# Products of the weighted sum held back by one block, in a hybrid attention block on one core

## The chip, the cores and the metric

The kernel runs on one core of one Trainium2 chip. Its engines are TensorE (PE in the profile; its weight loads are PEld), VectorE (DVE), ScalarE (ACT), GpSimd (POOL), and SyncE (SP), which issues most DMAs. The metric is the device time of one execution in microseconds (us), as the median of several runs.

## The reference

One decoder layer over 1024 tokens of width 1024. Eight heads of stick-breaking attention and eight heads of multi-head latent attention (MLA) share an input projection and an output projection; then come a gated MLP with a causal convolution and a gated input embedding. All is computed to float32 accuracy. The change touches only the last step of both attentions, the weighted sum of the values:

```python
# stick-breaking, per 128-query block
weights = where(strict, exp(log_sigmoid(z) + log_keep_after), 0.0)
outs.append(einsum('bhqk,bkhd->bqhd', weights, v[:, :end]))
# MLA, per 128-query block
probs = softmax(where(causal, s, -inf), axis=-1)
outs.append(einsum('bhqk,bkhd->bqhd', probs, v[:, :end]))
```

## The kernel before

*Precision.* Float32 operands are split into a high part (rounded to the matmul's type by a copy on ScalarE, line 93) and a low part (the difference, on VectorE, line 94), and matmuls of the parts are added up in PSUM. In the tile names an ending h or l tells them apart: th and tl are the high and low part of a transposed block of weights.

*Stages.* Up to 111 us the input is normed and the first projections are made. From 111 to 409 us runs the stick-breaking attention, from 409 to 691 us the MLA attention. After that come the second half of the output projection, the MLP and the embedding.

*Units.* Each attention is cut into 16 units: one head (e tells the two heads of a pair apart) and one half g of the queries, 512 of them, that is four query tiles of 128. A unit of half g has 4g + 4 key blocks of 128, so 4 or 8 blocks; the 16 stick-breaking units have 96 blocks together, as have the MLA units. The scores and weights of a unit (`sb_softmax`, `ml_softmax`) are made four query tiles w[i] at a time, one per step. In the stick-breaking attention a step has a scan on VectorE (line 649) and a product (line 651), in MLA a reduction (line 1078) and an exponential (line 1079).

*The weighted sum.* `weighted_sum` goes over the key blocks j of a unit. For each it transposes the weights of up to four query tiles on TensorE into one PSUM bank with the tag "tr" (line 461; there are two such banks), splits the bank into th and tl (lines 93 and 94), and adds two products, of v(j) with th and with tl (lines 475 and 476), to the PSUM tile av, of which there is one buffer. The transposes of block j + 1 are issued ahead of the products of block j. v(j) holds the high parts of 64 value columns beside the low parts, so that av has two halves. At the unit's end the halves are added: line 479 copies the lower half into tmp, line 481 adds the upper half and writes o. In MLA the reciprocal sums are spread over a "tr" bank, rb, by eight small matmuls (line 487), line 489 adds the halves and line 490 multiplies into o. tmp has the tag "tl" and so shares the two buffers of tl. A post function then issues the store of o on POOL's queue (line 680 for the stick-breaking pairs, line 1096 in MLA).

*What runs beside it.* `run_units` advances the softmax of the next unit by the blocks of the present one, and each block also calls `prepare.step()` (splitting of MLA keys, values and queries) and `fill.step(rate)`, which issues a piece of a list of filler work: the next pair's projections, the preparation of MLA (lines 576 to 582 copy its keys and values through the tile lt and store them), output projection, embedding, MLP.

*What sets the order.* The kernel is written in a framework that gives each instruction a priority from its place in the program and places all waits itself. A planner then lays out each engine's queue with modelled durations: an engine takes, among the instructions that are ready by the plan, the one with the lowest priority number. Filler work can be given a later priority by the numbers in `LATER`. On the chip each queue runs in the order of that plan.

Of the kernel before, what the change touches and what calls it, by code (L numbers as in the profile page):

```python
# [9 lines left out]
F32 = mybir.dt.float32  # L10
F32R = mybir.dt.float32r
I32 = mybir.dt.int32
AF = mybir.ActivationFunctionType
ALU = mybir.AluOpType
# [4 lines left out]
P = 128  # L19
# [4 lines left out]
H = 512  # L24
HD = 64
# [24 lines left out]
def tile_hybrid_block(ctx: ExitStack, tc: tile.TileContext, a: dict, out: bass.AP):  # L50
    nc = tc.nc
    act, dve, pool, pe, sp = nc.scalar, nc.vector, nc.gpsimd, nc.tensor, nc.sync
# [16 lines left out]
    ident_r = const.tile([P, P], F32R, name="ident_r")  # L69
# [16 lines left out]
    def nm(s):  # L86
        uid[0] += 1
        return f"{s}_{uid[0]}"

    def split(h, l, src, gain=None, on_pool=False):  # L90

        if gain is None:
            act.copy(h, src)  # L93
            (pool if on_pool else dve).tensor_tensor(l, src, h, ALU.subtract)  # L94
        else:
            act.activation(h, src, AF.Copy, scale=gain)
            dve.scalar_tensor_tensor(l, src, gain, h, ALU.mult, ALU.subtract)
# [97 lines left out]
    now = {}  # L195
# [83 lines left out]
    with tc.tile_pool(name="pre", bufs=1) as pre, \  # L279
# [155 lines left out]
        for _ in project(8, to_v(pairs[0]), (1,), vws):  # L435
# [3 lines left out]
    atb = sb_scope.enter_context(tc.tile_pool(name="attn_b", bufs=1, side="right",  # L439
                                              reuse_waits="tile"))  # L440
# [10 lines left out]
    def weighted_sum(u, p_, ptr, pav, rate):  # L451

        g, w, v = u["g"], u["w"], u["v"]
        av = pav.tile([P, H], F32, tag="av", name=nm("av"))
        last = 4 * g + 3

        def transposed(j):
            tr = one_bank(ptr, "tr")
            for i in range(max(4 * g, j), last + 1):
                c = (i - 4 * g) * P  # L460
                pe.transpose(tr[:, c:c + P], w[i][:, j * P:(j + 1) * P], ident)  # L461
            return tr

        nxt = transposed(0)
        for j in range(last + 1):
            lo = max(0, j - 4 * g) * P
            tr = nxt
            th = p_.tile([P, H], F32R, tag="th", name=nm("th"), bufs=2)
            tl = p_.tile([P, H], F32R, tag="tl", name=nm("tl"), bufs=2)
            split(th[:, lo:], tl[:, lo:], tr[:, lo:])  # L470
            if j < last:
                nxt = transposed(j + 1)
            prepare.step()
            fill.step(rate)
            pe.matmul(av[:, lo:], v(j), th[:, lo:], start=j == 0, stop=False)  # L475
            pe.matmul(av[:, lo:], v(j), tl[:, lo:], start=False, stop=j == last)  # L476
            yield
        t_ = p_.tile([HD, H], F32, tag="tl", name=nm("tmp"), bufs=2)
        act.copy(t_, av[HD:, :])
        if "rs" not in u:  # L480
            dve.tensor_tensor(u["o"], av[:HD, :], t_, ALU.add)
            return

        rb = one_bank(ptr, "tr")
        for i in range(4):
            for m, r in enumerate(u["rs"]):
                pe.matmul(rb[:HD, i * P:(i + 1) * P], r[:, i:i + 1].to_broadcast([P, HD]), ident_r,
                          start=m == 0, stop=m == 1)
        dve.tensor_tensor(t_, av[:HD, :], t_, ALU.add)
        dve.tensor_tensor(u["o"], t_, rb[:HD, :], ALU.mult)  # L490

    def run_units(units, softmax, p_, ptr, pav, rates):

        def start(u):
            u["pre"](u)
            return softmax(u)

        for _ in start(units[0]):
            pass
        for n, u in enumerate(units):  # L500
            nxt = start(units[n + 1]) if n + 1 < len(units) else iter(())
            per = 4.0 / (4 * u["g"] + 4) * AHEAD
            credit = 0.0
            for _ in weighted_sum(u, p_, ptr, pav, rates[u["g"]]):
                credit += per
                while credit >= 1.0:
                    credit -= 1.0
                    next(nxt, None)
            for _ in nxt:
                pass  # L510
            if u.get("post"):
                u["post"](u)


    def psum(name, bufs, side="left"):
# [3 lines left out]
    def one_bank(pool_, tag):  # L519
        return pool_.tile([P, H], F32, tag=tag, name=nm(tag))  # L520

    def cycle(makers):
        n = [0]

        def make():
            n[0] += 1
            return makers[(n[0] - 1) % len(makers)]()
        return make

    ptr = ctx.enter_context(tc.tile_pool(name="ptr", bufs=2, space=PSUM, reuse_waits="tile"))  # L530
    pav = ctx.enter_context(tc.tile_pool(name="pav", bufs=1, space=PSUM, reuse_waits="tile"))
# [1 line left out]
    x_cm, px = psum("px", 2)  # L533
    y_cm, py = psum("py", 2, "right")
    now["bank"] = cycle([lambda: one_bank(ppj, "pj")] + [lambda: one_bank(px, "pj")] * 2)
    now["tmp"] = lambda dt: atb.tile([P, H], dt, tag="lt", name=nm("lt"), bufs=4)

    def latent_t(j, th, lh, ll):
        src = tmp().rearrange("p (t c) -> p t c", t=4)
# [403 lines left out]
    with tc.tile_pool(name="mla", bufs=1, side="right", reuse_waits="tile") as ml:  # L943
# [20 lines left out]
        def load_q(pr):  # L964
            g, c = pr // 4, pr % 4
            t = mt("qld", [P, 4, 2 * QW], F32, 2)
            sp.dma_start(t, q_dram[c, :, 4 * g:4 * g + 4, :])
            loads["q", pr] = t

        def load_k(pr):  # L970
            g, c = pr // 4, pr % 4
            n = (g + 1) * H
            for e in range(2):
                t = mt("ld", [P, S], F32, 3)
                sp.dma_start(t[:HD, :n], k_dram[c, e * HD:(e + 1) * HD, :n])
                if 2 * pr + e - 8 * g < 3:
                    sp.dma_start(t[HD:QW, :n], kr_dram[:, :n])
                loads["k", 2 * pr + e] = t
# [8 lines left out]
        def make_k(n):  # L987
            t = loads.pop(("k", n))
            g = n // 8
            rows = QW if n - 8 * g < 3 else HD  # L990
            w = (g + 1) * H
            h, l = kts[n % 3]
            act.copy(h[:rows, :w], t[:rows, :w])
            yield
            pool.tensor_tensor(l[:rows, :w], t[:rows, :w], h[:rows, :w], ALU.subtract)
            yield

        def make_v(n):
            t = loads["v", n // 2]
            e, j = n % 2, 4 * (n // 8) + 4  # L1000
            z = ml.tile([P, NT, P], F32R, tag="v", name=nm("v"), bufs=3)
            src = t[:, :j, e * HD:(e + 1) * HD]
            act.copy(z[:, :j, :HD], src)
            pool.tensor_tensor(z[:, :j, HD:], src, z[:, :j, :HD], ALU.subtract)
            vs_[n] = z
            yield

        def make_q(n):
            t = loads["q", n // 2]
            e = n % 2  # L1010
            h, l = [mt("q" + x, [P, H], F32R, 2) for x in "hl"]
            ps = ptr.tile([P, H], F32, tag="tr", name=nm("tr"))
            for i in range(4):
                pe.transpose(ps[:QW, i * P:(i + 1) * P], t[:, i, e * QW:(e + 1) * QW], ident)
            act.activation(h[:QW], ps[:QW, :], AF.Copy, scale=MLA_SCALE)
            dve.scalar_tensor_tensor(l[:QW], ps[:QW, :], MLA_SCALE, h[:QW], ALU.mult,
                                     ALU.subtract)
            qs_[n] = (h, l)
            yield

        def ml_pre(u):
            n, e = u["n"], u["e"]
            pr = n // 2
            prepare.drain()
            if e == 0:
                ml_pre.o = ml.tile([P, H], F32, tag="o", name=nm("o"), bufs=2)
                for z in (n, n + 1):
                    prepare.add(make_v(z))
                if pr < 7:
                    load_k(pr + 1)  # L1030
                    load_q(pr + 1)
            elif pr < 7:
                for z in (n + 1, n + 2):
                    prepare.add(make_k(z))
            if n < 15:
                prepare.add(make_q(n + 1))
            if e == 1 and pr < 7:
                load_v(pr + 1)
            u["k"], u["q"] = kts[n % 3], qs_[n]
            u["v"] = lambda j: vs_[n][:, j, :]  # L1040
            u["out"] = ml_pre.o
            u["o"] = ml_pre.o[hs[e], :]
            g = u["g"]
            first = n == 0
            u["w"] = {i: (mq if first else ml).tile([P, (i + 1) * P], F32, tag=f"w{i % 4}",
                                                    name=nm(f"w{i}"), bufs=1 if first else 2)
                      for i in range(4 * g, 4 * g + 4)}
            if n == 8:
                y_cm[0].__exit__(None, None, None)
                y_cm[0], py_[0] = psum("py2", 1, "right")  # L1050
# [201 lines left out]
    for t in range(NT):  # L1252
# [7 lines left out]
        for n, (c0, c1) in enumerate(zip(cuts, cuts[1:])):  # L1260
            w = c1 - c0
            dh, o = c0 // 512, c0 % 512
# [19 lines left out]
        r = rstd_dve(rp, ssq[:, 0:1], D, 1, "rn", 4)  # L1282
# [65 lines left out]
```

## Time and profile before

| | |
|---|---|
| median of 3 runs | 1577.84 us (1576.06 to 1579.86) |
| the profiled execution | 1584.88 us, span 1583.1 us |
| TensorE busy | 1479.8 us, 93% of the span |
| VectorE busy | 1075.7 us, 68% |
| ScalarE busy | 841.2 us, 53% |
| mean granted TensorE clock | 0.978 |
| transposes of line 461 | 576, 102.6 us |
| products of lines 475 and 476 | 192 and 192, 78.5 and 77.2 us |
| th on ScalarE, tl on VectorE | 192 each, 91.0 and 103.2 us |

The profile is of one execution. Its times count from the span's start. A row of busy times by stretch gives the stretch, its length, and for each engine busy us and instructions, then the granted TensorE clock (1 is full speed), the DMA engines' share and GB/s. A row of waits names the waiting instruction by engine, tile and line, then what ended the wait, the total us, how many times, and the longest. A row in order of time gives the start, the duration, engine, line, operation, out<-in, shape and count, and in brackets the idle time of the engine before it with what ended it. A row of a group of one line gives minimum, median and maximum in ns and the first and last start in us; one of the groups by cost gives busy us and mean ns, then idle us before them.

### The profile page before, as it was taken

The page shows a single profiled execution, that of the slowest core. Times are in us where ns is not written, and L with a number is a line of the kernel's source. Part 1 is how long each engine was busy: PE and PEld are TensorE (multiplying, and loading weights), DVE is VectorE, ACT ScalarE, POOL GpSimd, SP SyncE. Part 2 cuts the span into 40 slices and gives each one's busy share as a digit, 9 for nine tenths or more (in the row PEclk, how much of TensorE's full clock was granted, in tenths as well). Part 3 has the DMA queues.
Part 4 walks back from the last instruction along what each step waited for, and adds up shares of the span by engine and source line. Part 5 has one row for each costly group of instructions (what it writes and reads, how often), then busy time and mean ns, then how long its engine had stood idle before and what let it go on. Part 6 is the DMA issues. An engine that isn't in the chain of part 4 may idle for free. (4 is left out here: it accounts for less than half of the span.)

```text
span 1583.1 us, 20827 instructions
## 1 busy us (share of the span) xinstructions
PE 1479.8 (93%) x7032; PEld 1212.8 (77%) x7032; DVE 1075.7 (68%) x2021; ACT 841.2 (53%) x1649; POOL 279.1 (18%) x319
## 2 busy tenths in 40 slices
PE   4998998987899898899999999999999999999996
PEld 3977886865678676777888788888888888888875
DVE  4559477899777767866658855445976656444798
ACT  5356465677777675655544544444544444444542
POOL 7106300002243334241114000000000000000033
PEclk9999999999899899999999999999999999999998
DMA  6031310113444424234435532223432222233354
GB/s 197 22 100 41 106 35 14 47 53 126 143 139 148 130 90 157 67 110 145 150 117 191 169 103 88 99 93 99 152 122 94 93 94 96 92 95 97 127 178 168
DMA packets 109212, 173.78 MB, mean 110 GB/s; under 512 B 10913, under 2 KB 47681, under 8 KB 109105
## 3 DMA queue, kind: packets, MB, share of 16 engines
q1 hardware_dynamic: 100400, 142.71, 28.7%
q0 software_dynamic: 8704, 29.74, 5.1%
q8 instruction: 55, 0.90, 0.2%
q14 instruction: 53, 0.43, 0.1%
HBM read 142.26 MB, written 30.15 MB: 109 GB/s over the span
## 5 line engine op out<-in xcount | busy, mean ns | idle before, releaser
L94 DVE TENSOR_TENSOR wl<-ws,wh 128x512 fp32r<-128x512 f32 x281 | 203.9, 727 | 147.4 <-ACT wh L93 84.2
L93 ACT CAST wh<-ws 128x512 fp32r<-128x512 f32 x296 | 182.9, 620 | 219.6 <-PE mm L897 103.4
L897 PE MATMUL mm<-bh,wh 128*128 128x512 f32 x456 | 180.1, 395 | 0.0
L895 PE MATMUL mm<-bh,wh 128*128 128x512 f32 x456 | 180.1, 395 | 0.0
L94 DVE TENSOR_TENSOR fl<-f,fh 128x512 fp32r<-128x512 f32 x88 | 60.8, 692 | 117.9 <-PE mm L118 77.4
L94 DVE TENSOR_TENSOR tl<-tr,th 128x512 fp32r<-128x512 f32 x192 | 103.2, 550 | 45.3 <-ACT th L93 41.8
L901 PE MATMUL mm<-bh,wl 128*128 128x512 f32 x456 | 126.0, 396 | 0.0
L93 ACT CAST th<-tr 128x512 fp32r<-128x512 f32 x192 | 91.0, 485 | 59.6 <-PE tr L461 49.5
L93 ACT CAST fh<-f 128x512 fp32r<-128x512 f32 x88 | 54.6, 622 | 110.0 <-PE mm L117 84.4
L1166 POOL DMA_DIRECT2D x_dram<-fd x8 | 4.3, 538 | 616.9 <-DVE fd L1165 584.0
L461 PE MATMUL tr<-ident,w 128*128 128x128 f32 x576 | 102.6, 286 | 10.5 <-DVE tl L94 5.7
L895 PEld LDWEIGHTS mm<-bh,wh 128*128 128x128 f32 x456 | 85.9, 188 | 19.9
L897 PEld LDWEIGHTS mm<-bh,wh 128*128 128x128 f32 x456 | 85.9, 188 | 19.8
L901 PEld LDWEIGHTS mm<-bh,wl 128*128 128x128 f32 x456 | 85.6, 188 | 19.8
L649 DVE TENSOR_TENSOR_SCAN kc<-kc,one_f 128x128 f32<-128x128 f32 (+3 forms) x64 | 88.0, 1381 | 13.1 <-ACT kc L646 12.9
L116 PE MATMUL mm<-wh,fh 128*128 128x512 f32 x242 | 95.6, 396 | 0.0
L476 PE MATMUL av<-tl,v 128*128 128x512 f32 x192 | 77.2, 404 | 19.4 <-DVE tl L94 18.1
L117 PE MATMUL mm<-wl,fh 128*128 128x512 f32 x242 | 95.3, 394 | 0.0
L461 PEld LDWEIGHTS tr<-ident,w 128*128 128x128 f32 x576 | 73.9, 146 | 26.4 <-DVE tl L94 8.6
L475 PE MATMUL av<-th,v 128*128 128x512 f32 x192 | 78.5, 409 | 12.9 <-ACT th L93 7.6
L118 PE MATMUL mm<-wh,fl 128*128 128x512 f32 x242 | 82.5, 395 | 0.0
L116 PE MATMUL pj<-hTh,wh 128*128 128x512 f32 x160 | 65.6, 410 | 0.0
(425 smaller groups left out, 3808.2 us busy)
## 6 DMA issues: line engine op xcount, KB each, us to landing
ws<-in_w_up SPq DMA_DIRECT2D x176, 256.0 KB, 2.6
ws<-in_w_down SPq DMA_DIRECT2D x88, 256.0 KB, 2.6
ws<-in_w_o SPq DMA_DIRECT2D x32, 256.0 KB, 2.8
xl<-x_dram SPq DMA_DIRECT2D x16, 512.0 KB, 4.1
ws<-in_w_in SPq DMA_DIRECT2D x24, 256.0 KB, 2.9
t<-o_dram SPq DMA_DIRECT2D x24, 256.0 KB, 3.2
xl<-o_dram SPq DMA_DIRECT2D x24, 256.0 KB, 2.9
xt<-in_x SPq DMA_DIRECT2D x8, 512.0 KB, 6.0
```

The costliest lines, as they stand in the source:

```text
L93: act.copy(h, src)
L94: (pool if on_pool else dve).tensor_tensor(l, src, h, ALU.subtract)
L116: pe.matmul(ps, lh, rh, start=start, stop=False)
L117: pe.matmul(ps, lh, rl, start=False, stop=False)
L118: pe.matmul(ps, ll, rh, start=False, stop=stop)
L461: pe.transpose(tr[:, c:c + P], w[i][:, j * P:(j + 1) * P], ident)
L475: pe.matmul(av[:, lo:], v(j), th[:, lo:], start=j == 0, stop=False)
L476: pe.matmul(av[:, lo:], v(j), tl[:, lo:], start=False, stop=j == last)
L649: dve.tensor_tensor_scan(rev, rev, one_f[:, 0:1].to_broadcast([P, n]), 1.0, ALU.mult, ALU.mult)
L895: pe.matmul(ps, wh[:, k * P:(k + 1) * P], nh[:, kk], start=kk == 0, stop=False)
L897: pe.matmul(ps, wh[:, k * P:(k + 1) * P], nl[:, kk], start=False, stop=False)
L901: pe.matmul(ps, wl[:, k * P:(k + 1) * P], nh[:, kk], start=False, stop=kk == NK - 1)
```

## The change

The products of block j are no longer issued in the step of block j. They are put into a list `held` and issued in the step of the next block, after that block's split, after the transposes of block j + 2, and after `prepare.step()` and `fill.step(rate)`. This goes across units: the products of a unit's last block, and with them the unit's end and its post function, are issued in the first step of the next unit, and those of the last unit after the loop. The tile av is taken only after that. th gets a third buffer; for the room, lt goes from four buffers to three and the MLA tile o from two to one.

```diff
 def weighted_sum(u, p_, ptr, pav, rate):
-    av = pav.tile([P, H], F32, tag="av", name=nm("av"))
...
+    def product(j, lo, th, tl):
+        pe.matmul(av[:, lo:], v(j), th[:, lo:], start=j == 0, stop=False)
+        pe.matmul(av[:, lo:], v(j), tl[:, lo:], start=False, stop=j == last)
+        if j == last:
+            finish()
+
+    def finish():
+        t_ = p_.tile([HD, H], F32, tag="tl", name=nm("tmp"), bufs=2)
+        act.copy(t_, av[HD:, :])
+        if "rs" not in u:
+            dve.tensor_tensor(u["o"], av[:HD, :], t_, ALU.add)
+        else:
+            rb = one_bank(ptr, "tr")
+            for i in range(4):
+                for m, r in enumerate(u["rs"]):
+                    pe.matmul(rb[:HD, i * P:(i + 1) * P], r[:, i:i + 1].to_broadcast([P, HD]),
+                              ident_r, start=m == 0, stop=m == 1)
+            dve.tensor_tensor(t_, av[:HD, :], t_, ALU.add)
+            dve.tensor_tensor(u["o"], t_, rb[:HD, :], ALU.mult)
+        if u.get("post"):
+            u["post"](u)
+
     nxt = transposed(0)
     for j in range(last + 1):
...
-        th = p_.tile([P, H], F32R, tag="th", name=nm("th"), bufs=2)
+        th = p_.tile([P, H], F32R, tag="th", name=nm("th"), bufs=3)
         tl = p_.tile([P, H], F32R, tag="tl", name=nm("tl"), bufs=2)
         split(th[:, lo:], tl[:, lo:], tr[:, lo:])
         if j < last:
             nxt = transposed(j + 1)
         prepare.step()
         fill.step(rate)
-        pe.matmul(av[:, lo:], v(j), th[:, lo:], start=j == 0, stop=False)
-        pe.matmul(av[:, lo:], v(j), tl[:, lo:], start=False, stop=j == last)
+        if held:
+            held.pop()()
+        if j == 0:
+            av = pav.tile([P, H], F32, tag="av", name=nm("av"))
+        held.append(lambda a=(j, lo, th, tl): product(*a))
         yield
...
+held = []
 def run_units(units, softmax, p_, ptr, pav, rates):
...
-        if u.get("post"):
-            u["post"](u)
+    held.pop()()
...
-now["tmp"] = lambda dt: atb.tile([P, H], dt, tag="lt", name=nm("lt"), bufs=4)
+now["tmp"] = lambda dt: atb.tile([P, H], dt, tag="lt", name=nm("lt"), bufs=3)
...
-            ml_pre.o = ml.tile([P, H], F32, tag="o", name=nm("o"), bufs=2)
+            ml_pre.o = ml.tile([P, H], F32, tag="o", name=nm("o"), bufs=1)
```

More of the change, by code (lines that the diff above doesn't have):

```diff
@@ L474, in weighted_sum @@
             fill.step(rate)
-            pe.matmul(av[:, lo:], v(j), th[:, lo:], start=j == 0, stop=False)
-            pe.matmul(av[:, lo:], v(j), tl[:, lo:], start=False, stop=j == last)
-            yield
[L478 to L490, printed above, removed]
+            if held:
[3 more added lines that the diff above has]
+            held.append(lambda a=(j, lo, th, tl): product(*a))
+            yield
+    held = []
     def run_units(units, softmax, p_, ptr, pav, rates):
```

## The prediction

> **What bounds the kernel now.** I read the page's busy times first, then the busy time by stage, then the waits of TensorE in the two attention stages, then the rows in order of time around typical waits.
>
> ```profile
> PE 1479.8 (93%) x7032; PEld 1212.8 (77%) x7032; DVE 1075.7 (68%) x2021; ACT 841.2 (53%) x1649; POOL 279.1 (18%) x319
> ```
>
> ```profile
> core 0: us, PE busy (x) PEld busy (x) DVE busy (x) ACT busy (x) POOL busy (x), PEclk, DMA share, GB/s
> 111.00:409.00 298.00, 267.66 (x1369) 219.45 (x1368) 236.53 (x313) 187.96 (x415) 53.14 (x79) 0.95 0.17 57
> 409.00:691.00 282.00, 251.81 (x1414) 210.87 (x1414) 207.15 (x390) 189.23 (x404) 105.30 (x93) 0.95 0.40 125
> 260.00:280.00 20.00, 15.74 (x68) 12.76 (x69) 12.86 (x19) 9.36 (x19) 0.00 (x0) 0.83 0.08 26
> 355.00:396.00 41.00, 31.49 (x155) 23.52 (x153) 40.94 (x53) 28.98 (x66) 12.18 (x17) 0.92 0.35 126
> ```
>
> TensorE is the bound. The change touches only the stick-breaking stage (111 to 409 us) and the MLA stage (409 to 691). There TensorE idles 298.00 − 267.66 = 30.3 and 282.00 − 251.81 = 30.2 us, 60.5 together, and its granted clock is 0.95, so some 0.05 × 580 = 29 us more go to half-rate stretches. So all that can be won is idle and slow clock in these 580 us; filler matmuls moved about win nothing, since their total stays. From 355 to 396 us VectorE is busy 40.94 of 41 us: there it is the bound.
>
> ```profile
> engine line waited for: us in total, times, longest us
> PE av L476 <- DVE tl L94: 12.2, 18, 1.4
> PE tr L461 <- DVE tl L94: 5.0, 4, 2.1
> PE av L475 <- DVE o L481: 4.7, 2, 2.3
> PE av L475 <- ACT th L93: 0.3, 1, 0.3
> ...
> PE av L475 <- ACT th L93: 7.3, 5, 2.0
> PE av L476 <- DVE tl L94: 5.9, 8, 2.5
> PE tr L461 <- DVE o L490: 1.6, 2, 0.9
> PE tr L461 <- DVE tl L94: 0.7, 2, 0.4
> ...
> PE av L476 <- DVE tl L94: 4.3, 6, 1.4
> PE av L475 <- DVE o L481: 2.3, 1, 2.3
> PE tr L461 <- DVE tl L94: 0.9, 1, 0.9
> ```
>
> The waits of TensorE: four rows of 111 to 409, four of 409 to 691, three of 355 to 396 (part of the first). The first eight are the weighted sum's own: 12.2 + 5.0 + 4.7 + 0.3 = 22.2 and 7.3 + 5.9 + 1.6 + 0.7 = 15.5, so **37.7 of the 60.5 us**. Of these 4.3 + 2.3 + 0.9 = 7.5 lie where VectorE is full, and I leave them where they are.
>
> ```profile
> 378.66 0.60 PE L461 MATMUL tr<-ident,w 128*128 128x128 f32 x4
> 379.01 0.48 PE L475 MATMUL av<-th,v 128*128 128x512 f32 x1
> 379.75 0.66 DVE L94 TENSOR_TENSOR tl<-tr,th 128x512 fp32r<-128x512 f32 x1
> 380.46 0.50 PE L476 MATMUL av<-tl,v 128*128 128x512 f32 x1 [0.97 <-DVE tl L94]
> 380.79 0.60 PE L461 MATMUL tr<-ident,w 128*128 128x128 f32 x4
> ```
>
> One block in order of time. The product of th at 379.01 already stands behind the next block's transposes (378.66); the product of tl waits 0.97 us for VectorE (380.46), and the transposes of the block after that follow at 380.79. They need the same tl, since there are two "tr" banks and tl is the last reader of one. So whichever comes first on TensorE's queue takes the wait.
>
> **The change part by part.**
>
> *Product one block later.* Nothing is added or removed on any engine: 2 products, 4 (or fewer) transposes, one th and one tl per block as before; the program's order decides a priority, and the planner lays each engine's queue out by its own durations. What changes where TensorE waits for tl: the transposes of block j+2 go at once when tl(j) is there, and the products of block j stand behind them. The loop transposes, th, tl, transposes gets shorter by the slot that the product had in front: 380.79 − 380.46 = 0.33 us. Outside the full stretch there are 18 + 8 − 6 = 20 such waits, together 12.2 + 5.9 − 4.3 = 13.8 us: 20 × 0.33 = **−6.6 us** (bounds: 0, if only the name of the waiter changes, and −13.8, if the wait is wholly covered). The five waits for th in MLA (7.3 us) go the same way, as the next step needs tl too: 5 × 0.33 = **−1.7 us** (0 to −7.3).
>
> *The unit's end one block later, across units.*
>
> ```profile
> 262.46 2.28 DVE L649 TENSOR_TENSOR_SCAN kc<-kc,one_f 128x1024 f32<-128x1024 f32 x1
> 262.60 0.44 PE L461 MATMUL tr<-ident,w 128*128 128x128 f32 x2 [1.76 <-DVE tl L94]
> 264.66 0.66 DVE L481 TENSOR_TENSOR o<-av,tmp 64x512 f32<-64x512 f32 x1
> 265.37 0.80 PE L475 MATMUL av<-th,v 128*128 128x512 f32 x1 [2.33 <-DVE o L481]
> ```
>
> There is one av bank. The next unit's first product waits until o has read it, and o stood behind a scan of 2.28 us on VectorE: 2.33 us idle. The change puts the first product a block later, but the copy, the addition and (in MLA) the eight reciprocal matmuls come a block later too, behind the next unit's first split. Of the 4.7 − 2.3 = 2.4 us of such waits outside the full stretch, and of the 1.6 for L490, where rb holds a "tr" bank that the next unit's second block now gets first, I take three quarters: **−3 us** (bounds: −4.0, all of it; above, the second rival's +2.33 a unit end).
>
> *Clock.* Idle falls by 11.3 of 60.5 us, 19%; the same share of 29 us would be 5.4. The granted clock falls in steps (0.83 in 260 to 280, with 4.1 us of idle close together), so small gains may free none: I take half, **−3 us** (0 to −5.4).
>
> The Trainium skill, "TensorE: Matmul & The Clock Gate", section "Why this matters for your kernels", asks for no idle gap over some 3 us to keep the full clock. The longest wait here is 2.5 us, so by that rule alone the clock term would be 0 and the forecast 1571; the trace disagrees, with 0.83 around waits of 1.76 and 2.33 us.
>
> *The room for a third th buffer.* "lt" goes from 4 buffers to 3, MLA's "o" from 2 to 1.
>
> ```profile
> L581 DVE COPY lt<-pj x8: 656/680/684, 349.8 to 375.4; 128x512 f32<-128x512 f32 x8
> L576 ACT COPY lt<-pj x8: 578/614/658, 349.9 to 375.4; 128x512 f32<-128x512 f32 x8
> DMA to landing us min/median/max: 1.9/2.8/5.2
> ...
> L1096 POOL DMA_DIRECT2D o_dram<-o x8: 557/558/590, 436.9 to 692.8; - x8
> ...
> DMA to landing us min/median/max: 2.3/2.4/4.1
> ```
>
> Sixteen copies into lt in 25.6 us, 1.6 us apart. A slot is held for copy, issue and landing, about 0.68 + 0.56 (as the issue of o below) + 2.8 = 4.0 us, so three slots give one per 1.3 us: enough in the mean, not at the longest landing. It lies in the stretch where VectorE is full, and the work ends 33 us before the stage does: **+1 us** (0 to +3). MLA's o is stored 8 times, landing after 2.4 us (at most 4.1), and is written next about a unit later, 282 / 16 = 17.6 us: **0**; without that cover 8 × 2.4 = 19 us would be at stake, but it would need POOL to hang 13 us.
>
> *"tl" keeps two slots, which tmp shares.* At a unit's end tl(0) of the next unit and tmp hold both; tl(1) waits for o, now emitted after tl(0). Behind tl(1) on VectorE stand the next score reductions or scans, and ScalarE and TensorE wait for those.
>
> ```profile
> L481 DVE TENSOR_TENSOR o<-av,tmp 64x512 f32<-64x512 f32 x16 | 10.9, 678 | 1.5 <-ACT tmp L479 1.3
> ...
> L489 DVE TENSOR_TENSOR tmp<-av,tmp 64x512 f32<-64x512 f32 x16 | 10.9, 679 | 3.5 <-ACT tmp L479 3.5
> ```
>
> VectorE idled 1.5 + 3.5 = 5.0 us before these 32 operations, the first that each unit's end puts on it. A little over half of that again is added: **+3 us** (0 to +5.0; the rival has more).
>
> *Stores and the queues.* POOL issues the stores of o a block later; the fillers that unit 7 of MLA adds come a block later too. The last product and end of each of the two runs were the tail of them before as well. Nothing waits for these: **0**, bounded by one block in each run, 298 / 96 = 3.1 us.
>
> Sum: −6.6 − 1.7 − 3 − 3 + 1 + 3 = **−10.3 us**. The profiled execution took 1584.9 us (span 1583.1 and 1.8 around it) and would take 1574.6. It is 7.0 above the median of the three runs, 1577.84, so for the median I say **1568**.
>
> **The rivals.**
>
> *The wait only changes its name (no change).* Products already stand behind the next block's transposes (378.66 before 379.01), the transposes need the same tl, and where the planner has something else ready it puts it there in both versions. For it: the two "tr" banks are as they were, and the chain is bound by VectorE and ScalarE. Against it: the 2.33 us at 265.37 are not of that kind. Then only the clock's noise and lt's +1 stay: 1575 to 1580.
>
> *The later end blocks the next unit (slower).* Place: o on VectorE at each of the 32 unit ends. It is now emitted behind the last scores of the next unit and its first split, so more often a scan like that of 262.46 is put in front of it; the av bank, both tl slots and, in MLA, one "tr" bank hang on it. Price: 2.33 us for each, as at 265.37. Against the gains without that term, 6.6 + 1.7 + 3 − 1 = 10.3, it decides from 10.3 / 2.33 = 5 more unit ends on. If ten are hit: +23 − 10 = +13, so 1591; with seven, 1584.
>
> The Trainium skill, "TensorE: Matmul & The Clock Gate", "Architectural detail", says that VectorE and ScalarE are strictly first in, first out, so an o placed behind a scan cannot pass it. The trace agrees: o starts at 264.66, where the scan of 262.46 with 2.28 us ends.
>
> *The queue gets real slack (much faster).* If a block of delay covers all of 37.7 − 7.5 = 30.2 us, half of the 60.5, and the clock follows with half of its 29: −45, so 1533; half of that success is 1555. For it: waits of 0.4 to 2.5 us against a block of 3 us. Against it: the transposes' need of tl.
>
> **How the numbers follow.** A measurement of this kernel tells a change from none at about 0.2%, 3.2 us. The forecast (3 to 20 us faster, 1558 to 1575) gets 0.42, no change 0.20, the blocked unit ends 0.28, real slack 0.10. Faster is 0.42 + 0.10 = 0.52, within 0.2% 0.20, slower 0.28. The range leaves out the outer parts of the last two, about 0.1 each: 1552 to 1588.
>
> **What would show it.** Right: the waits of av for tl and th in the two stages fall from 26 and 6 to a few, some return as tr waiting for tl, and the sum of the eight rows falls from 37.7 to about 26; idle from 60.5 to about 50; clock 0.96. Products stand behind two later transposes rather than one. The name-change rival shows as tr waiting for tl by as much as av lost. The unit-end rival shows as av or tr waiting for o, or VectorE's tl waiting for o, in more than five unit ends. The forecast is wrong if the planner's new order moves fillers so that waits appear at lines which the change doesn't touch, or if lt's lost buffer is missed and waits of pj for lt take the place of those of av.

## The result, and the profile after

The changed kernel takes 1591.38 us in the median of four runs (1590.11 to 1604.27), the kernel before 1577.76 us (four runs, 1576.06 to 1579.86). The ratio is 1.0105, with a 95% interval of 1.0079 to 1.0131: **slower by 13.6 us**, where 10 us faster was forecast. The profiled execution took 1590.11 us, span 1588.3.

Busy time by stage, after (columns as before):

```profile
core 0: us, PE busy (x) PEld busy (x) DVE busy (x) ACT busy (x) POOL busy (x), PEclk, DMA share, GB/s
111.00:409.00 298.00, 263.27 (x1349) 217.12 (x1347) 231.09 (x311) 185.04 (x412) 54.23 (x79) 0.96 0.18 58
409.00:691.00 282.00, 247.48 (x1412) 206.87 (x1412) 208.77 (x392) 188.69 (x402) 100.08 (x90) 0.95 0.41 126
260.00:280.00 20.00, 15.91 (x75) 13.03 (x74) 11.25 (x16) 9.76 (x20) 0.00 (x0) 0.91 0.09 26
```

TensorE's idle time in the two stretches is now 34.7 and 34.5 us, 69.2 instead of 60.5. It should have fallen to about 50. The attention's last product starts earlier than before (682.2 instead of 689.1), but between 111 and 691 us TensorE was busy for 8.7 us less, with 22 matmuls fewer by the counts in the rows. So less filler was done beside the attention, and it comes after.

Over the whole execution the page gives

```profile
PE 1474.5 (93%) x7032; PEld 1210.6 (76%) x7032; DVE 1075.9 (68%) x2021; ACT 840.6 (53%) x1649; POOL 279.4 (18%) x319
```

that is 1588.3 − 1474.5 = 113.8 us idle against 1583.1 − 1479.8 = 103.3: 10.5 us more, with the same number of instructions on every engine. This one execution is only 5.2 us longer than that of before, because TensorE was 5.3 us less busy. Half of that is explained: it spent 65.0 us of its span at half rate, instead of 70.5, which is 2.7 us less of work lost. Where the other half comes from is not shown.

The four runs of the changed kernel have granted clocks of 0.980, 0.970, 0.979 and 0.974; the mean is 0.976, while the 79 runs of the kernel before that stand beside the experiments have a mean of 0.979. Time times one minus the clock estimates what half rate costs: 38.7 and 32.9 us. So of the difference of the means of these runs, 1594.3 − 1578.3 = 16 us, **about 6 is half-rate clock and about 10 is idle** by this estimate. The 6 hang on the one run at 0.970; the other three alone give 2.6.

The waits of TensorE, after, from 111 to 409 us and then from 409 to 691:

```profile
engine line waited for: us in total, times, longest us
PE tr L460 <- DVE tl L94: 15.2, 18, 2.2
PE av L464 <- DVE o L473: 6.8, 5, 2.3
PE pj L116 <- DVE v L94: 3.9, 2, 2.1
PE pj L116 <- ACT qt L620: 3.3, 2, 3.0
...
PE sc L656 <- ACT w L661: 1.8, 3, 1.3
...
PE tr L460 <- DVE tl L94: 7.3, 5, 2.2
PE tr L460 <- ACT w L1093: 3.3, 2, 2.0
PE sc L1084 <- ACT qh L1029: 3.2, 4, 2.6
PE av L464 <- ACT th L93: 3.2, 3, 1.4
PE sc L1084 <- ACT w L1093: 3.0, 4, 1.5
```

The products' waits for tl (18.1 us in 26 waits over both stretches) are nearly gone. The transposes now wait 15.2 + 7.3 = 22.5 us for the same tl, where they waited 5.0 + 0.7 before: **the wait changed its name**. In sum over all waits for tl of the weighted sum it is 23.8 us before (18.1 + 5.7) and 24.0 after (22.5, with 0.7 at the products and 0.8 at the reciprocal matmuls). The wait for o grew from 4.7 us (2 times) to 6.8 (5 times), the wait for th fell from 7.6 to 3.2. What else is new stands at lines that the change doesn't touch. With the rows of the two stages added up by kind, the scores waited 2.9 us in all and now 8.0, the fillers 13.6 and now 15.7, the transposes for w 2.7 and now 5.1.

One block in order of time, after (rows left out):

```profile
380.69 0.66 DVE L94 TENSOR_TENSOR tl<-tr,th 128x512 fp32r<-128x512 f32 x1
381.41 0.66 PE L460 MATMUL tr<-ident,w 128*128 128x128 f32 x4 [0.75 <-DVE tl L94]
381.82 0.49 PE L465 MATMUL av<-tl,v 128*128 128x512 f32 x1
382.15 0.40 PE L464 MATMUL av<-th,v 128*128 128x512 f32 x1
```

tl of 380.69 is waited for by the transposes that want its bank (0.75 us). The product at 381.82, right behind them, takes the same tl: counted in order, both are the 78th of 192. In the block shown of before, the product of the awaited tl stood first and had the wait (0.97 us). So a block later in the program is not a block later on the chip. In the median a product with tl starts 1.45 us after the end of its tl, where it started 0.96 us after it before.

VectorE's waits from 111 to 691 us, before and then after:

```profile
DVE mx L1078 <- PE sc L449: 10.9, 10, 2.2
...
DVE tl L94 <- PE av L476: 2.5, 2, 1.5
```

```profile
DVE mx L1092 <- PE sc L449: 15.5, 20, 3.0
...
DVE tl L94 <- PE av L465: 6.5, 6, 2.6
```

VectorE's reductions wait for scores twice as often. tl waits 6.5 us (6 times) for the held product that still reads its slot; before that was 2.5 us (2 times).

A unit's end, the first one of the stick-breaking attention, in order of time. First before, then after:

```profile
124.31 0.58 ACT L479 COPY tmp<-av 64x512 f32<-64x512 f32 x1
126.20 0.68 DVE L481 TENSOR_TENSOR o<-av,tmp 64x512 f32<-64x512 f32 x1
...
134.21 0.39 PE L475 MATMUL av<-th,v 128*128 128x512 f32 x1
```

```profile
132.59 1.13 ACT L93 CAST th<-tr 128x512 fp32r<-128x512 f32 x2
...
134.46 0.68 DVE L94 TENSOR_TENSOR tl<-tr,th 128x512 fp32r<-128x512 f32 x1
134.73 0.58 ACT L471 COPY tmp<-av 64x512 f32<-64x512 f32 x1
...
137.07 0.67 DVE L473 TENSOR_TENSOR o<-av,tmp 64x512 f32<-64x512 f32 x1
...
137.80 0.80 PE L464 MATMUL av<-th,v 128*128 128x512 f32 x1 [1.59 <-DVE o L473]
```

The last product of this unit ended at about the same time in both (it started at 123.21 before and at 123.74 after). Before, the end was over by 126.9 and the next unit's first product found av free 7 us later. After, tmp stands behind the next unit's split. That split had to wait for the next unit's weights, so av stayed taken until 137.7. Over the stick-breaking units tmp starts 4.15 us after the start of the unit's last product in the mean (0.90 before), in MLA, its last unit left out, 2.31 (1.05).

### The profile page after: what moved, and what is told of

Same layout as the page of the kernel before. It is cut to its first block, busy times and chain, and to the rows that moved or that the text cites. A ratio compares the mean times of both kernels' runs of the same rounds, so it can differ in the third digit from the quotient of the medians.

```text
span 1588.3 us, 20883 instructions
## 1 busy us (share of the span) xinstructions
PE 1474.5 (93%) x7032; PEld 1210.6 (76%) x7032; DVE 1075.9 (68%) x2021; ACT 840.6 (53%) x1649; POOL 279.4 (18%) x319
## 5 line engine op out<-in xcount | busy, mean ns | idle before, releaser
L460 PEld LDWEIGHTS tr<-ident,w 128*128 128x128 f32 x576 | 70.3, 145 | 51.6 <-DVE tl L94 33.5
L663 DVE TENSOR_TENSOR_SCAN kc<-kc,one_f 128x128 f32<-128x128 f32 (+3 forms) x64 | 87.3, 1369 | 13.1 <-ACT kc L660 12.8
L464 PE MATMUL av<-th,v 128*128 128x512 f32 x192 | 73.8, 384 | 11.9 <-DVE o L473 6.8
```

Of the source, the lines that this page charges most:

```text
L663: dve.tensor_tensor_scan(rev, rev, one_f[:, 0:1].to_broadcast([P, n]), 1.0, ALU.mult, ALU.mult)
```

## The experiments

Theories after the result. *Blocked unit ends*: the loss is the later unit end. *Later products inside a unit*: the loss is the place of the product behind two blocks' transposes. *Buffers*: it is lt, o, th or the slots. *Planner's scatter*: any reordering of these queues by the planner costs this much, whatever it is for. The expectations call the first two theory 1 and theory 2, and the last one theory 3. Each run has five rounds, beside runs of the kernel before on the same chip; a difference is between the two medians. What half rate costs is estimated each time as above, from the means of time times one minus the clock.

**Delay inside the units alone.** The unit's last products and its end are issued in their old place.

```diff
             held.append(lambda a=(j, lo, th, tl): product(*a))
+            if j == last:
+                held.pop()()
             yield
```

> The delay inside a unit alone: the last block's products and the unit's end are issued in the unit's own last step again; the third th buffer and the lost lt and o buffers stay. Theory 1 (the loss comes from the unit's end, which waits for the next unit's first split): the loss of 13.6 us goes, and what is left is the delay inside the unit, between 0 and -7 us: 1571 to 1578. The copy tmp starts about 1 us after a unit's last product (before 0.90 and 1.05 us in the mean, after 4.15 and 2.31). Theory 2 (the delay itself lengthens the wait, since the transposes take it over): still 8 to 14 us slower, 1586 to 1592, with tr waiting for tl by some 22 us. Theory 3 (any new order of the planner costs about as much): anywhere from 1575 to 1592.

Measured: 1590.18 against 1577.02, **+13.2 us**, ratio 1.0096 (1.0074 to 1.0118). tmp starts 1.02 and 1.10 us after the start of the last product, close to before. The whole loss is there without one late unit end, so blocked ends are not needed for it. Its runs have a mean clock of 0.9745 against 0.979, so more than half of this loss, 7.7 us, is half-rate clock.

**Delay across the unit ends alone.** Every product but a unit's last is issued at once.

```diff
             held.append(lambda a=(j, lo, th, tl): product(*a))
+            if j < last:
+                held.pop()()
             yield
```

> The delay at the unit's end alone: only the products of a unit's last block, and the unit's end, go into the next unit's first step; all other products are issued in their own step as before. Theory 1: the whole loss stays, 1588 to 1594, the copy tmp starts 2 to 4 us after a unit's last product, and av waits for o by about 7 us. Theory 2: close to the kernel before, 1576 to 1580, and TensorE waits for tl at the products again. Theory 3: anywhere from 1575 to 1592.

Measured: 1595.57, **+18.6 us**, ratio 1.0124 (1.0103 to 1.0144). So this half loses too, and the halves don't add up: 13.2 + 18.6 = 32 against 13.6 for both. The clock is part of it: with a mean of 0.973, some 10 of the 18.6 us are half rate. What the rest is made of was not taken apart.

**The buffers alone.** The kernel before with

```diff
-    now["tmp"] = lambda dt: atb.tile([P, H], dt, tag="lt", name=nm("lt"), bufs=4)
+    now["tmp"] = lambda dt: atb.tile([P, H], dt, tag="lt", name=nm("lt"), bufs=3)
-                ml_pre.o = ml.tile([P, H], F32, tag="o", name=nm("o"), bufs=2)
+                ml_pre.o = ml.tile([P, H], F32, tag="o", name=nm("o"), bufs=1)
```

> The kernel before with lt at three buffers and the MLA tile o at one; no product moves. Theories 1 and 2: within 2 us of before, 1576 to 1580. If the lost buffers make the loss: 1586 to 1592, with pj waiting for lt, or o for its store. Theory 3: up to 8 us away, as far as the planner's order changes.

Measured: 1582.56, **+5.5 us**, ratio 1.0030 (1.0015 to 1.0044).

**Buffers, taken apart: lt alone.** o with one buffer leaves the planned queues as they are, row by row, so only lt was run: the first two lines of the diff above.

> The kernel before with lt at three buffers alone; the MLA tile o keeps two. The queues are those of the run with both lost buffers, row by row, so if that run's 5.5 us come from lt: 1580 to 1585 again, and if they come from o's store at run time: 1575 to 1579.

Measured: 1583.13 against 1579.32, **+3.8 us**, ratio 1.0025 (1.0010 to 1.0041). The copies through lt are spread wider. Before:

```profile
L581 DVE COPY lt<-pj x8: 656/680/684, 349.8 to 375.4; 128x512 f32<-128x512 f32 x8
```

and with lt 3:

```profile
L581 DVE COPY lt<-pj x8: 661/678/692, 349.8 to 379.3; 128x512 f32<-128x512 f32 x8
```

The last copy comes 3.9 us later from the same start. So the room for the third th slot has a price of about 4 us in the kernel before.

**The whole delay with the buffers of before.** The changed kernel, and lt and o as in the lines with a minus above.

```diff
-            th = p_.tile([P, H], F32R, tag="th", name=nm("th"), bufs=3)
+            th = p_.tile([P, H], F32R, tag="th", name=nm("th"), bufs=2)
```

> The whole delay, inside units and across them, with the buffers of before: lt at four, the MLA tile o at two, th at two. The lost buffers alone cost 5.5 us, and the changed kernel 13.6. Theory 2 (two additive parts, the buffers and the order): 8 us slower than before, 1585, with TensorE's wait for tl at the transposes instead of the products. Theory 1 (all of the order's loss at the unit's end): the same 8 us, but with av waiting for o more than before's 4.7 us. If the third th buffer matters: 1590 or more.

Measured: 1592.21 against 1579.32, **+12.9 us**, ratio 1.0080 (1.0057 to 1.0104). Against the +13.6 of the changed kernel no difference can be seen: either the third th slot wins back what the lost lt slot costs, or the 4 us of lt are not added on top of the delay. No run tells these apart.

**tmp gets a buffer of its own** (the changed kernel, th with two).

```diff
-            t_ = p_.tile([HD, H], F32, tag="tl", name=nm("tmp"), bufs=2)
+            t_ = p_.tile([HD, H], F32, tag="tm", name=nm("tmp"), bufs=1)
```

> The changed kernel with a buffer of its own for tmp, for which th goes back from three buffers to two. Theory 1, in the form that tmp is held up because it takes its turn at the two tl slots behind the next unit's tl(0): tmp starts about 1 us after the last product, the second split of a unit no longer waits for o, and 6 to 12 us come back: 1579 to 1585. If the lateness lies in the program's order and not in the slots: 1588 to 1594, and tmp still starts 2 to 4 us late. Theory 2: no change against the changed kernel, 1588 to 1594.

Measured: 1586.71, **+9.7 us**, ratio 1.0059 (1.0044 to 1.0073). The same unit end as above:

```profile
123.34 0.58 ACT L471 COPY tmp<-av 64x512 f32<-64x512 f32 x1
125.22 0.68 DVE L473 TENSOR_TENSOR o<-av,tmp 64x512 f32<-64x512 f32 x1
...
133.48 0.39 PE L464 MATMUL av<-th,v 128*128 128x512 f32 x1
```

tmp no longer stands behind the next split, and the first product waits for nothing. In the mean over the stick-breaking units tmp starts 1.20 us after the start of the last product, and a unit's tl(1) starts 0.33 us after its tl(0) has ended, instead of 3.59 (1.57 in the kernel before). So the late end has a cause, the slots that tmp shares with tl, in which it takes its turn by place in the program. Mending it wins back 13.6 − 9.7 = 3.9 us of the loss, not all, and less than the 6 to 12 expected. The two differences come from separate comparisons, and th has two buffers here instead of three, so the 3.9 is rough.

**Two reorderings with no purpose.** The kernel before, first with the next unit's softmax advanced faster, then with other filler rates. The expectations count moved rows in the planned queue. In the traces, outside the longest order that each shares with the kernel before, stand 277 of TensorE's 7032 matmuls in the first and 804 in the second, against 825 in the changed kernel.

```diff
-AHEAD = 0.9
+AHEAD = 1.0
```

> The kernel before with the softmax of the next unit advanced a little faster (1.0 instead of 0.9 of a step per quarter of the unit); no product moves in the program, but the planner moves 518 of TensorE's 6326 rows. Theory 3 (the loss comes from any new order, since the numbers of before suit its own order): 3 to 12 us slower, 1580 to 1589, with waits spread over many lines. Theories 1 and 2 say nothing on it; within 3 us of before, 1574 to 1580, would speak against theory 3.

```diff
-SB_RATE = 0.75
-ML_RATE = (1.2, 0.8)
+SB_RATE = 0.7
+ML_RATE = (1.1, 0.7)
```

> The kernel before with fillers issued a little more slowly (0.70 instead of 0.75 per block in the stick-breaking stage, 1.1 and 0.7 instead of 1.2 and 0.8 in MLA); no product moves in the program, the planner moves 1091 of TensorE's rows, as many as the change does (1436). Theory 3: 3 to 12 us slower, 1580 to 1589. Within 3 us of before, 1574 to 1580, would speak against theory 3.

Measured: 1577.06 and 1578.15 against 1579.32, −2.3 and −1.2 us, ratios 0.9984 (0.9966 to 1.0001) and 0.9990 (0.9976 to 1.0005). In these two runs moving up to as many rows costs nothing, so a reordering by the planner does not cost this much whatever it is for.

**Inside the units, with the buffers of before.** As the first run, with th, lt and o as in the whole delay with the buffers of before.

> The delay inside a unit alone, with all buffers of before (th two, lt four, o two). Theory 2 (the transposes take over the wait for tl, so nothing is won, and the queue behind them gets worse): the run with the lost buffers was 13 us slower, of which lt's is 4 to 5; so 6 to 10 us slower, 1585 to 1589. TensorE's waits for tl together (at products and transposes) stay at 22 to 26 us, most of it at the transposes. Theory 1 (all of the loss at the unit's end): within 3 us of before, 1576 to 1582.

**The same, with the held product ahead of the next transposes.**

```diff
         split(th[:, lo:], tl[:, lo:], tr[:, lo:])
+        if held:
+            held.pop()()
         if j < last:
             nxt = transposed(j + 1)
         prepare.step()
         fill.step(rate)
-        if held:
-            held.pop()()
```

> As the run before it, but the held product is issued ahead of the next block's transposes instead of behind them and the fillers: the delay reaches over the softmax step and the next split alone. Theory 2: close to the kernel before, 1576 to 1582, with TensorE's waits for tl at the products again. If the delay over the split is what costs (ScalarE and VectorE rather than TensorE): as slow as the run before it, 1585 to 1589.

Measured, on one chip: 1594.19 and 1582.27 against 1578.41, **+15.8 and +3.9 us**, ratios 1.0102 (1.0078 to 1.0127) and 1.0030 (1.0012 to 1.0047). Waits of TensorE from 111 to 691 us, first behind and then ahead of the transposes:

```profile
PE tr L460 <- DVE tl L94: 18.8, 26, 2.5
PE sc L1085 <- ACT qh L1030: 6.9, 5, 5.7
PE av L464 <- ACT th L93: 6.2, 7, 1.6
PE av L464 <- DVE o L473: 5.9, 3, 2.3
PE av L465 <- DVE tl L94: 4.9, 8, 1.5
```

```profile
PE av L465 <- DVE tl L94: 18.7, 24, 2.4
PE tr L460 <- DVE tl L94: 5.6, 5, 2.1
PE av L464 <- DVE o L473: 4.8, 3, 2.3
...
PE av L464 <- ACT th L93: 2.9, 7, 0.7
...
PE sc L1085 <- ACT qh L1030: 1.7, 2, 1.6
```

The waits for tl are 18.8 + 4.9 = 23.7 and 18.7 + 5.6 = 24.3 us: equal, with the names exchanged. The 12 us lie elsewhere. All of TensorE's waits here are 68.5 and 56.9 us; 6.0 of the 11.6 between them are the scores' (10.3 and 4.3) and 3.3 are the products' for th. In the slower kernel the scores wait 6.9 us for qh alone, once 5.7, and VectorE's reductions wait for them:

```profile
DVE mx L1093 <- PE sc L449: 24.4, 18, 5.2
```

```profile
DVE mx L1093 <- PE sc L449: 15.2, 14, 2.7
```

These two kernels differ in one place in the program. If the product is put behind the transposes but ahead of `prepare.step()` and `fill.step(rate)`, the planned queues are those of the first of the two, row by row. So **it is the place behind the next transposes that costs, and the filler's place doesn't matter**. The clock changes little here: of the 12 us some 2 are half rate.

**A third tl slot.** The first run, and

```diff
-        th = p_.tile([P, H], F32R, tag="th", name=nm("th"), bufs=3)
-        tl = p_.tile([P, H], F32R, tag="tl", name=nm("tl"), bufs=2)
+        th = p_.tile([P, H], F32R, tag="th", name=nm("th"), bufs=2)
+        tl = p_.tile([P, H], F32R, tag="tl", name=nm("tl"), bufs=3)
```

> The delay inside a unit, with th at two buffers and tl at three, lt at three and o at one; the same with th at three and tl at two was 13.2 us slower than before. If the two tl slots are what binds (VectorE's in-order queue stands while a put-back product still holds one): 5 to 10 us come back, 1581 to 1586, and VectorE's wait of tl for products goes to about 0. If not: 1588 to 1595 as there.

Measured: 1590.59 against 1578.41, +12.2 us, ratio 1.0081 (1.0066 to 1.0096), where the first run had +13.2. VectorE's wait of tl for products, 3.8 us in the first run, is gone, and the loss is still there. So VectorE's wait for a slot that the held product still reads is not what costs.

**A third "tr" bank in the stick-breaking stage**, taken from the three banks of the fillers, in the kernel before and with the whole delay (buffers of before). Every third "tr" tile goes to pz; the lines of the class that does this are left out.

```diff
-    x_cm, px = psum("px", 2)
+    x_cm, px = psum("px", 1)
+    z_cm, pz = psum("pz", 1)
...
-    run_units(units, sb_softmax, atb, ptr, pav, (SB_RATE, SB_RATE))
+    run_units(units, sb_softmax, atb, Three(), pav, (SB_RATE, SB_RATE))
```

> The kernel before with a third tr bank in the stick-breaking stage, taken from the fillers' banks (three to two there). It is the reference for the next run. The fillers lose a bank, so 0 to 10 us slower, 1578 to 1588; the waits of products for tl in that stage fall a little from 12.2 us, and those of transposes for tl (5.0 us) go.

> The whole delay with the buffers of before, with a third tr bank in the stick-breaking stage. Theory 2 says that the delay fails there because the transposes need the same tl as the products, for want of a third bank: in that stage the waits for tl then fall by half or more against the reference run with three banks, and idle there is 4 us or more below that of the run with the delay and two banks (33.9 us). In the MLA stage nothing changes, so the whole is still slower than its reference, by 2 to 8 us. If the waits for tl in the first stage do not fall: the bank is not what binds, and the loss is that without the third bank, some 13 us.

Measured: 1588.93 and 1599.21 against 1578.41, +10.5 and +20.8 us, ratios 1.0063 (1.0040 to 1.0086) and 1.0131 (1.0109 to 1.0152). The fillers' lost bank costs 10.5 by itself, and the delay still costs 10.3 on top of it. By the clocks (means of 0.976 and 0.971) some 7.6 of these 10.3 are half rate. Waits in the stick-breaking stage, without and then with the delay:

```profile
PE av L476 <- DVE tl L94: 8.5, 12, 1.4
PE tr L461 <- DVE tl L94: 5.8, 6, 1.9
```

```profile
PE av L465 <- DVE tl L94: 7.7, 14, 1.1
...
PE tr L460 <- DVE tl L94: 6.2, 5, 1.6
```

14.3 and 13.9 us. The third bank takes 17.2 (12.2 + 5.0) down to 14.3, but with it the delay hides none of the rest. It does change who waits: with the delay and two banks the transposes had 13.4 us of such waits, with three they have 6.2, and the products 7.7. These products wait for their own tl and start 0.06 us after it, so the planned queue puts no block between a tl and its product here either. The lack of a third bank is not why the delay wins nothing.

**One stage alone** (inside the units, buffers of before): stick-breaking, then MLA.

```diff
-            if j == last:
+            if j == last or "n" in u:        # stick-breaking alone
+            if j == last or "n" not in u:    # MLA alone
                 held.pop()()
```

> The delay inside a unit with the buffers of before, in the stick-breaking stage alone; the MLA units issue each product in its own step. Idle of TensorE rose by 1 us in that stage and by 8.5 in MLA in the run with both, so: 2 to 6 us slower than before, 1580 to 1584. If each stage pays half: 1585 to 1588.

> The delay inside a unit with the buffers of before, in the MLA stage alone. By the idle of the run with both: 9 to 14 us slower than before, 1587 to 1592, with scores and fillers waiting 8 us or more longer in that stage. If each stage pays half: 1585 to 1588.

Measured: 1587.01 and 1579.10 against 1578.41, **+8.6 and +0.7 us**, ratios 1.0051 (1.0034 to 1.0068) and 1.0007 (0.9996 to 1.0017). Their sum, 9.3, is less than the 15.8 of both. It was expected the other way round, with most of the loss in MLA. TensorE's row from 409 to 691 us, MLA alone and then both:

```profile
409.00:691.00 282.00, 252.21 (x1419) 209.68 (x1420) 207.46 (x390) 187.67 (x399) 105.90 (x94) 0.95 0.41 126
```

```profile
409.00:691.00 282.00, 243.34 (x1380) 202.75 (x1380) 205.18 (x387) 186.01 (x396) 96.20 (x86) 0.95 0.39 123
```

The same MLA code idles 29.8 us behind the old stick-breaking stage and 38.7 behind the delayed one; the old MLA code behind the delayed stage idles 282.00 − 249.93 = 32.1. So what the delay costs in MLA depends on what the planner carries over from the stage ahead. **What stays open** is the carrier of the 15.8 − 9.3 = 6.5 us that the two stages cost only together, and of the scores' longer waits. The runs show that the loss comes with the product behind two blocks' transposes, and more from the stick-breaking stage, but not which planned instruction carries it; no run held the MLA queue equal while the stage ahead of it changed.

## Why the prediction was wrong, point by point

**The product one block later (−6.6 and −1.7 forecast).** This is the step that failed first. It took it that a loop of transposes, th, tl, transposes gets shorter by the product's slot of 0.33 us. The waits for tl stayed at 23.8 and 24.0 us, so not one slot was won there; only th's wait fell, by 4.4 us, more than the 1.7 expected. The rival "the wait only changes its name" describes this part exactly, and the prediction had its evidence in hand: the products of th stood behind the next transposes already, and both consumers wait for the same tl. Its reason, the two "tr" banks, explains who waits (13.4 us at the transposes with two, 6.2 with three) but not that nothing is won, as the run with three banks shows.

**What the longer delay costs inside a unit.** No step had a price for it: "nothing is added or removed on any engine" was taken as the bound from above, 0. It measured +13.2 to +15.8 us, half-rate clock included, and +3.9 with the product ahead of the transposes. The prediction did name what would make it wrong, waits at lines that the change doesn't touch. That is what happened: scores, transposes for w and fillers together 19.2 us before (2.9 + 2.7 + 13.6) and 28.8 after (8.0 + 5.1 + 15.7). Which planned instruction brings these waits about stays open.

**The unit's end (−3 forecast).** The wait for o rose from 4.7 to 6.8 us. The rival of blocked ends had the right sign, and its 1591 for ten ends is what was measured; but only five ends wait for o, by 6.8 us in all, and the loss is there without late ends. Its size agrees by coincidence, its mechanism is a part: delayed ends alone cost 18.6 − 5.5 = 13.1 us over the buffers, if these add up, and in the whole change tmp's shared slots cost some 3.9. Its place was half right: o is late less because of a scan than because tmp, ahead of it, waits for the next split. The Trainium skill, "TensorE: Matmul & The Clock Gate", "Architectural detail", which has VectorE and ScalarE strictly first in, first out, bears on this. The trace agrees in the order: ScalarE made the two casts of 132.59 first and tmp at 134.73. Whether tmp was ready earlier it doesn't show.

**tl's two slots, which tmp shares (+3, 0 to +5).** Right in kind, and in size as far as the rough 3.9 us tell.

**lt (+1, 0 to +3) and o (0).** lt was too small: +3.8 alone, above its bound of +3, though the interval (some 1.6 to 6.5 us) covers that; the longest landing of 5.2 us, which the prediction saw that three slots don't cover, may be why, but no run tells that apart. Nothing speaks against 0 for o: 5.5 us with both buffers lost and 3.8 with lt's alone have intervals that overlap.

**Clock (−3).** The sign was wrong in the mean of the runs: about +6 us, 2.6 without the slowest run. That the clock's loss goes with the idle time is not borne out: in the profiled execution idle rose by 10.5 us and the time at half rate fell by 5.5, and with the third tl slot the loss of 12.2 us came at the clock of before (0.979). The rule that the prediction weighed (the Trainium skill, "TensorE: Matmul & The Clock Gate", "Why this matters for your kernels"), no idle gap over some 3 us, is too mild after the change as well:

```profile
126.67 0.44 PE L460 MATMUL tr<-ident,w 128*128 128x128 f32 x2 [1.39 <-DVE w L665]
```

```profile
120.00:127.20 7.20, 5.36 (x32) 4.38 (x32) 7.09 (x9) 5.58 (x14) 0.00 (x0) 1.00 0.00 0
127.20:130.70 3.50, 3.50 (x14) 3.37 (x13) 3.50 (x4) 0.48 (x1) 0.47 (x1) 0.51 0.00 0
130.70:134.00 3.30, 3.29 (x19) 2.70 (x17) 3.05 (x6) 3.06 (x8) 3.30 (x5) 1.00 0.00 0
```

One wait of 1.39 us, with 7.20 − 5.36 = 1.84 us of idle in the 7.2 us up to the row's end, is followed by a stretch at half rate in which TensorE is never idle. The kernel before has the same wait of 1.39 us at 126.34 and half rate from 126.74.

**Real slack (1533 to 1555).** Nothing of it was seen. A product starts half a microsecond later behind its tl than before (1.45 instead of 0.96 us in the median), not a block later.

## What to carry to other kernels

To move a consumer behind the next producer on an in-order queue wins nothing when that producer waits for the same result: count who else waits for it, and add those rows before and after. Check in the trace, too, how much later the consumer really runs, since a planner may undo most of a later place in the program. A later consumer is not free even if it stalls nowhere itself; here it cost 12 us against the same delay placed ahead of the transposes, in good part through waits of scores that nobody had touched. A temporary that shares slots with the pipelined tile takes its turn among them, so a later unit end puts it behind the next unit's work; and before a loss is put down to a planner's reshuffling, reshuffle the kernel before by as much and time that.

## What the runs showed of the hardware that was not expected

Half rate, a granted clock of 0.5, comes in multiples of one length. All 17 pieces of the profiled execution before and 16 after last 3.41 us or twice that, but for the one at the very end of each (7.71 and 9.01), and sum to 72.6 and 67.0 us; in the run across the unit ends alone one lasts 23.89, seven times as long. Each piece but the last begins after 3.41 us in which TensorE idled 1.18 us or more in sum, not all at once. Other stretches of 3.41 us with up to 1.74 us of idle stayed at full clock, so idle of this size does not decide it alone. So waits of little more than a microsecond can cost 1.7 us of work beside themselves (half of 3.41). Whether they do varies between runs: one and the same kernel had granted clocks of 0.970 to 0.980 in four runs, and 1604.27 us at the 0.970.
